# A gated mixing block on one Trainium2 core: the last plain columns of the input projection join the two-by-two scheme, and x's sums of squares come from rows

## The chip, the core and the metric

The kernel runs on one core of a Trainium2 chip. Five engines work side by side, each through its own list of instructions in order: TensorE (PE) multiplies matrices into eight accumulation banks; VectorE (DVE) and ScalarE (ACT) do elementwise work; GpSimd (POOL) does elementwise work too; SyncE (SP) issues most of the loads. An instruction waits until the ones that it depends on, on other engines or in DMA queues, have signalled. The metric is the time of one execution in microseconds (us) on the device, as the median of several runs.

## The reference, cut to what matters

```python
h = rms_norm(x, norm_mix_g) * (1.0 + sc1) + sh1           # sc1, sh1 from silu(c) @ w_ada
proj = einsum('bsd,de->bse', h, w_in)                     # 1024 tokens, 1024 -> 7168 columns
b_s, c_s, v_s, v_c, gl_c, gate_br = split(proj, ...)
y_a = (b_s * causal_dwconv3(c_s * v_s)) @ w_short_out
u   = causal_dwconv31(v_c * sigmoid(gl_c)) + bias
y_b = silu(layer_norm(u)) @ w_conf_out
g_a, g_b = split(sigmoid(gate_br))
x = x + g1 * ((g_a * y_a + g_b * y_b) @ w_o)
x = x + g2 * swiglu(rms_norm(x) * ... )                   # then a last rms_norm
```

The change is in the first two lines: the norm of x, and the projection.

## The kernel before

Channels lie on partitions. x, h and all products are tiles of 128 channels by 512 tokens: eight chunks of channels, two halves of tokens (0 and 1). A weight matrix is cut into blocks of 128 by 128. fp32 values are split into a rounded part and a rest, and each block product takes three matmuls (`mm3`, lines 293, 294, 296): weight high by data high, weight high by data rest, weight rest by data high. `split_w` makes the parts of a weight tile: the cast on ACT (L211), the rest on DVE or POOL (L212). Three tiles of each part exist, so a weight tile can be split once the matmuls of the third tile before it are over. The first `WHOLE` = 3 chunks of the lead are multiplied as plain fp32 instead (L289).

Most of the projection goes through *duals*: two pairs of 128 columns at a time, as a two-by-two block scheme with seven products in place of eight (`PRODUCTS` = "1265734" gives their order). The blocks of the weights are named 11, 12, 21, 22 (first or second column of the pair, first or second four chunks of channels); those of h are the four chunks of either half and either half of the tokens. Product 1 is the first column by the first four chunks of token half 0, product 2 the same column by the last four; together they are that column's result on half 0. Products 6, 5, 7, 3, 4 work on sums of blocks. Every product of a dual is 2 pairs x 4 chunks x 3 = 24 matmuls. Three banks for each pair, x, y and z, take turns. The weights' block sums and their rests are made by POOL (L235 to L239, L212), the data's sums and splits by DVE and ACT (`t_split`, L332 and L333). `PAIRS` lists which columns make the pairs: "u" is a channel block of the convolution branch with its sigmoid gate, "p" a block of c_s and v_s, "q" one of b_s, "g" output gates.

Ahead of the twelve duals stands the *lead*: the three first "u" blocks and one gate column, seven columns in seven banks, by all eight chunks, on token half 0 and then on half 1 (`row_blocks`). `act_x` makes a chunk of h when it is due: two loads and reductions of the modulation weights ada (L274), the scale (L360), the shift and split (L364 to L372). After the lead one more gate column is done plainly (`col_block`, tile gb). The norm needs the sum of squares over channels, which lie on partitions: ACT squares each chunk, DVE adds the eight (L404, L408), and a matmul with ones sums over partitions into every row of a bank (L414); the inverse root is refined on 128x512 tiles (L343 to L350).

The order of the work is set by the program's order and a scheduler in the recording layer, within explicit constraints (`issue_after`). `plan` lists the weight tiles; `next_w` keeps `AHEAD` = 2 of them ready. Raw weights pass through five buffers; a load starts when the tile that held its buffer is used up, and SP issues loads in order. The 31-tap convolution is DVE work that is spread over the duals: `paced` ties every tap to a moment counted in products (`CONV_DUALS`). Tiles "uc" (eight, of a whole token length) hold u, p, sc and loads of ada; tiles "gs" (six half-wide ones) hold evacuated products. After the duals follow the y_a stage (the short branch's output projection, also in seven products), y_b, mix, the ffn and the last norm, whose code stays as it is but for the y_a stage's order.

Of the kernel before, what the change touches and what calls it, by code (L numbers as in the profile page):

```python
# [39 lines left out]
P = 128  # L40
# [24 lines left out]
LEAD = 7  # L65
WHOLE = 3


X1_AT = 5
# [14 lines left out]
CONV_DUALS = 10.8  # L84
MOD_DUALS = 9
AT_READS = {"7": 4.5, "3": 5.5, "4": 6.5}
# [25 lines left out]
def block_kernel(ctx: ExitStack, tc: tile.TileContext, x0, xT, c, vecs, ada, w_first, w_plain, w_duals,  # L112
# [63 lines left out]
    aff2 = cp.tile([P, KC], F32, name="aff2")  # L176
    wsum = cp.tile([P, CK // 2 * KC], F32, name="wsum")
# [22 lines left out]
    pool_los = []  # L200
# [4 lines left out]
    def split_w(raw, n, after=(), lo_engine=nc.vector):  # L205
        wh = whp.tile([P, 1024], F32R, tag="wh", name="wh")[:, :n]
        wl = wlp.tile([P, 1024], F32R, tag="wl", name="wl")[:, :n]
        with ExitStack() as order:
            for ins in after:
                order.enter_context(tc.issue_after(ins))  # L210
            nc.scalar.copy(wh, raw)  # L211
            lo = lo_engine.tensor_tensor(wl, raw, f32(wh), ALU.subtract)  # L212
        if n == T and lo_engine is nc.gpsimd:
            pool_los.append(lo.ins)
        return wh, wl

    def dual_units(mats, n, early=False, eng=nc.vector, lo=None):
# [6 lines left out]

        def unit(m):
            if early:
                get(*{"1": ("11",), "2": ("12",), "6": ("21", "22", "11"), "3": ("12",), "4": ("22",)}.get(m, ()))
            elif m == "1":
                get("11", "12", "21", "22")
            los = (lo or {}).get(m, eng)  # L230
            if m in "12":
                return split_w(a["1" + m], n, (), los)
            if m == "6":
                a["s1"] = a["22"] if early else raw_tile(n)
                eng.tensor_tensor(a["s1"], a["21"], a["22"], ALU.add)  # L235
                eng.tensor_tensor(a["21"], a["21"], a["11"], ALU.add)
                eng.tensor_tensor(a["11"], a["11"], a["s1"], ALU.add)
            elif m == "3":
# [3 lines left out]
        return {m: (lambda m=m: unit(m)) for m in PRODUCTS}  # L242


    plan = [None] * KC
    plan += [(w_plain[0], 1024)]
# [1064 lines left out]
```

## Time and profile before

| | us |
|---|---|
| median of 3 runs | 1485.38 (1481.1 to 1486.36) |
| the profiled execution | 1482.34 |
| its span | 1480.6 |
| first matmul of the lead | 18.74 |
| lead, token half 0 | 18.74 to 63.96 |
| lead, token half 1 | 63.96 to 102.05 |
| the plain gate column | 102.05 to 112.93 |
| twelve duals | 112.93 to 570.00 |

In a row of the timeline stand the start, the duration, the engine, the line, the operation, the tile written and the tiles read with their shape, and in brackets how long the engine stood idle before and what ended that. In a row of waits stand who waited for whom, the sum, the number of times and the longest. A row of windows gives the stretch, its length, then for PE, weight loads, DVE, ACT and POOL the busy time and the number of instructions, the clock granted to PE, the DMA engines' mean share and what they moved in GB/s. A row of one tile's view gives an operation's count and its shortest, median and longest duration in ns.

### The profile page before, as it was taken

What the parts mean: (1) busy time and instruction counts of PE and PEld (TensorE: products, weight loads), DVE (VectorE), ACT (ScalarE), POOL (GpSimd) and SP (SyncE); (2) the same over time, 40 slices, a digit from 0 to 9 for tenths busy, and PEclk for the clock granted to TensorE, in tenths of its full rate; (3) what the DMA queues carried; (4) which work ended last, traced back from release to release, by engine and by line L of the source; (5) the groups of instructions that cost most, each with busy time, mean ns of one, the idle gap of its engine ahead of it and who ended that gap; (6) DMA issues with size and microseconds to landing.
All of it is one profiled execution on the core that took longest, in us unless ns stands there. A gap on an engine that the chain in (4) does not pass through costs nothing.

```text
span 1480.6 us, 17737 instructions
## 1 busy us (share of the span) xinstructions
PE 1454.6 (98%) x6407; PEld 1189.3 (80%) x6407; DVE 1184.1 (80%) x1626; ACT 641.8 (43%) x926; POOL 528.1 (36%) x468
## 2 busy tenths in 40 slices
PE   6999999999999999999999999999999999999997
PEld 2788888888888888878888778888888888888887
DVE  7994999889999979989588699877676765677755
ACT  4663434444333346455336465444444443222235
POOL 0027777776877673110022001111000116545005
PEclk9999999999999999999999999999999999999999
DMA  9623223233322345575476338655444449998403
GB/s 351 219 75 100 91 89 120 93 107 122 107 71 72 107 133 201 200 221 189 159 262 210 118 107 264 238 187 177 140 158 145 139 156 351 375 298 269 157 4 114
DMA packets 84858, 247.78 MB, mean 167 GB/s; under 512 B 9761, under 2 KB 11937, under 8 KB 84770
## 3 DMA queue, kind: packets, MB, share of 16 engines
q1 hardware_dynamic: 40768, 134.24, 27.5%
q0 software_dynamic: 38096, 99.63, 20.3%
q10 hardware_dynamic: 5906, 12.78, 2.2%
q8 instruction: 50, 0.82, 0.2%
q14 instruction: 38, 0.31, 0.1%
HBM read 186.31 MB, written 60.29 MB: 167 GB/s over the span
## 4 chain that ended last, share of the span: by engine, by line
PE 86%; DVE 6%; issue 3%; DMA 2%; POOL 2%; ACT 0%; POOLq 0%; ACTq 0%; DVEq 0%
PE x L293 10%; PE x L294 10%; PE x L296 10%; PE z L294 7%; PE z L296 7%; PE z L293 7%; PE y L296 6%; PE y L294 6%; PE y L293 6%; PE yb L294 2%; PE mix L293 2%; PE yb L296 2%; PE mix L294 2%; PE mix L296 2%; PE yb L293 2%
## 5 line engine op out<-in xcount | busy, mean ns | idle before, releaser
L211 ACT CAST wh<-raw 128x1024 fp32r<-128x1024 f32 (+2 forms) x263 | 265.6, 1010 | 405.6 <-PE z L294 112.9
L212 POOL TENSOR_TENSOR wl<-raw,wh 128x1024 fp32r<-128x1024 f32 x85 | 209.7, 2471 | 108.4 <-ACT wh L211 108.4
L212 DVE TENSOR_TENSOR wl<-raw,wh 128x1024 fp32r<-128x1024 f32 (+2 forms) x178 | 204.4, 1149 | 49.5 <-ACT wh L211 47.9
L703 DVE SCALAR_TENSOR_TENSOR c<-diff,vec,c 128x512 f32<-128x512 f32 x248 | 176.6, 751 | 2.2
L1028 POOL DMA_DIRECT2D hid<-stage x71 | 37.8, 533 | 334.7 <-DVE stage L333 330.1
L293 PE MATMUL x<-th,wh 128*128 128x512 f32 x240 | 93.4, 389 | 0.0
L294 PE MATMUL x<-tl,wh 128*128 128x512 f32 x240 | 93.4, 389 | 0.0
L296 PE MATMUL x<-th,wl 128*128 128x512 f32 x240 | 93.4, 389 | 0.0
L703 DVE SCALAR_TENSOR_TENSOR c<-u,wsum,c 128x512 f32<-128x512 f32 x112 | 84.0, 750 | 2.0 <-ACT c L707 0.4
L332 ACT CAST stage<-g 128x512 fp32r<-128x512 f32 x62 | 38.4, 622 | 65.8 <-DMA hid<-stage 32.3
L293 PE MATMUL z<-th,wh 128*128 128x512 f32 x168 | 65.4, 389 | 0.0
L294 PE MATMUL z<-tl,wh 128*128 128x512 f32 x168 | 65.4, 389 | 0.0
L296 PE MATMUL z<-th,wl 128*128 128x512 f32 x168 | 65.4, 389 | 0.0
L235 POOL TENSOR_TENSOR raw<-raw 128x1024 f32<-128x1024 f32 x12 | 29.8, 2483 | 95.3 <-DVE wl L212 94.5
L333 DVE TENSOR_TENSOR stage<-g,stage 128x512 fp32r<-128x512 f32 x62 | 42.5, 689 | 24.4 <-ACT stage L332 24.4
L274 DVE CUSTOM_DVE_ANT_0 ada<-ada,cs,vec 128x1024 f32<-128x1024 f32 x33 | 49.0, 1500 | 9.0 <-DMA ada<-in_ada 9.0
L1054 POOL DMA_DIRECT2D th<-hid x71 | 38.1, 536 | 46.5 <-PE x L296 25.1
L293 PEld LDWEIGHTS x<-th,wh 128*128 128x128 f32 x240 | 45.0, 188 | 9.4
L296 PEld LDWEIGHTS x<-th,wl 128*128 128x128 f32 x240 | 45.0, 188 | 9.4
L294 PEld LDWEIGHTS x<-tl,wh 128*128 128x128 f32 x240 | 45.0, 188 | 9.2
L293 PE MATMUL y<-th,wh 128*128 128x512 f32 x132 | 51.3, 389 | 0.0
L294 PE MATMUL y<-tl,wh 128*128 128x512 f32 x132 | 51.3, 389 | 0.0
(923 smaller groups left out, 4273.5 us busy)
## 6 DMA issues: line engine op xcount, KB each, us to landing
hid<-stage POOLq DMA_DIRECT2D x71, 512.0 KB, 4.4
raw<-in_w_fi SPq DMA_DIRECT2D x53, 512.0 KB, 3.9
raw<-in_w_duals SPq DMA_DIRECT2D x48, 512.0 KB, 3.6
th<-hid POOLq DMA_DIRECT2D x71, 256.0 KB, 5.9
tl<-hid POOLq DMA_DIRECT2D x71, 256.0 KB, 6.2
ada<-in_ada SPq DMA_DIRECT2D x33, 512.0 KB, 5.3
raw<-in_w_fo SPq DMA_DIRECT2D x24, 384.0 KB, 6.2
raw<-in_w_conf SPq DMA_DIRECT2D x16, 512.0 KB, 4.4
```

The source lines that it names most:

```text
L211: nc.scalar.copy(wh, raw)
L212: lo = lo_engine.tensor_tensor(wl, raw, f32(wh), ALU.subtract)
L235: eng.tensor_tensor(a["s1"], a["21"], a["22"], ALU.add)
L274: nc.vector.tensor_tensor_reduce(out=raw, in0=raw, in1=cs, scale=1.0, scalar=col(V_ADA, b), op0=ALU.mult, op1=ALU.add, accum_out=modc(b),)
L293: nc.tensor.matmul(ps, wh, xh, start=first, stop=False, skip_group_check=again)
L294: nc.tensor.matmul(ps, wh, xl, start=False, stop=False, skip_group_check=again)
L296: mm3.ins = nc.tensor.matmul(ps, wl, xh, start=False, stop=last, skip_group_check=again).ins
L332: nc.scalar.copy(hi, src)
L333: t_split.ins = nc.vector.tensor_tensor(lo, src, f32(hi), ALU.subtract).ins
L703: tap.ins = nc.vector.scalar_tensor_tensor(out=out, in0=src[:, s : s + H], scalar=wt, in1=acc, op0=ALU.mult, op1=ALU.add).ins
L1028: nc.gpsimd.dma_start(hid_dram[key], s)
L1054: nc.gpsimd.dma_start(t, hid_dram[key][:, s])
```

## The change

All 28 column pairs now go through fourteen duals. The lead is no longer three whole "u" blocks and a gate but the *first columns* of the first seven pairs, and it runs on token half 0 alone. After four chunks the banks hold product 1: ACT copies them away (`m1_store`), those of dual 0 to tiles that stay, the others to DRAM; then the banks go on and hold products 1 + 2, which is the column's result on half 0 (`first_out`). Products 1 and 2 of the remaining first columns of duals 3 to 5 follow as products *ahead*, while the second half's norm and the block sums are made (`h1_pair`). A dual below 6 then copies its kept product 1 into its bank and runs only products 6, 5, 7, 3, 4. Its weights are loaded block by block when a product needs them (`early`), the block 22 a second time, since its buffer takes a sum.

For the norm a second copy of x, `xt`, comes with tokens on partitions. The sum of squares of a token is then a sum along a row that the squaring instruction gives itself (`row_square`): ACT does three of the four tiles of half 0, DVE one. The inverse root is made for four columns of 128 tokens, each column is spread to a diagonal matrix on ACT, and one matmul with ones puts it into every row of a bank (`row_spread`, `row_sum`), where the modulation reads it.

Also changed: the modulation loads of the duals are issued in duals 3 to 11 in place of 0 to 8; the convolution is paced from product 5 to 77.6 of 86 in place of 0 to 75.6 of 84; in the y_a stage an evacuation is issued only after the splits of the two next ready weight tiles, and two of the eight loads of the convolution's results come three products later.

```diff
-    ("p", 0), ("g", ("b", 2), ("b", 3)), ("p", 1), ("u", 3), ("q", 0), ...
+    ("u", 0), ("u", 1), ("u", 2), ("g", ("b", 0), ("b", 1)), ("p", 0), ("g", ("b", 2), ("b", 3)),
+    ("p", 1), ("g", ("b", 4), ("b", 5)), ("u", 3), ("g", ("b", 6), ("b", 7)), ("p", 2), ...
...
-CONV_DUALS = 10.8
+AHEAD_DUALS = 6
+CONV_FROM, CONV_TO = 5, 77.6
+MOD_FROM = 3
...
+    def row_square(h, i, t, act=True):
+        ss = rcol[h][0][:, i : i + 1]
+        if act:
+            return nc.scalar.activation(t, t, AF.Square, scale=1.0 / 32.0, accum_out=ss).ins
+        return nc.vector.tensor_tensor_reduce(
+            out=t, in0=t, in1=t, scale=1.0 / D, scalar=0.0, op0=ALU.mult, op1=ALU.add, accum_out=ss
+        ).ins
+    def row_spread(h, act):
+        ss, r, t = rcol[h]
+        with tc.issue_after(act):
+            nc.scalar.activation(r, ss, AF.Abs_reciprocal_sqrt, bias=eps1)
+        rstd_end(ss, eps1, r, t, None)
+        spread = g_tile("spread")
+        for i in range(H // P):
+            nc.scalar.activation(spread[:, i * P : (i + 1) * P], ident, AF.Copy, scale=r[:, i : i + 1])
+        return spread
+    def row_sum(spread):
+        bank = ps2_tile("rx")
+        nc.tensor.matmul(bank, ones, spread, start=True, stop=True)
+        return bank
...
+    def m1_store(d, p, ps):
+        t = hl_tile("m1", dt=F32)
+        m1_ins.append(nc.scalar.copy(t, ps).ins)
+        if d == 0:
+            m1[d, p] = t
+            return
+        m1_dram[d, p] = dram.tile([P, H], F32, name=f"m1_{d}{p}")
+        nc.scalar.dma_start(m1_dram[d, p], t)
...
+        xs, w = ops[k]
+        for o in range(LEAD):
+            mm3([lead[o]], slice(o * P, o * P + P), w, [xs], k == 0, k % KH == KH - 1, k >= KH)
+            if k == KH - 1:
+                m1_store(o // 2, o % 2, lead[o])
             elif k == KC - 1:
+                first_out(o // 2, o % 2, lead[o])
...
+    steps = [(d, m) for m in "12" for d in range(LEAD // 2, AHEAD_DUALS)]
+    for i, (d, m) in enumerate(steps):
+        if 0 < i <= KH:
+            h1_pair(i - 1)
+        w = next_w()
+        for p in range(d == LEAD // 2, 2):
...
+            (m1_store if m == "1" else first_out)(d, p, ahead[d, p])
+        if i == 0:
+            with tc.issue_after(mm3.ins):
+                rx_1 = row_sum(spread)
...
+        if d < AHEAD_DUALS:
+            for p in range(2):
+                nc.scalar.copy(x[p], m1[d, p])
+        for m in PRODUCTS[2 if d < AHEAD_DUALS else 0 :]:
...
+            with ExitStack() as order:
+                for ins in [e for r in ready[:2] for e in made[id(r[1])]]:
+                    order.enter_context(tc.issue_after(ins))
```

The lists of three engines show what moves. First ACT at the start, from its first square to the scale that releases the lead (sq and rx0r are the squares and the inverse root; rc are the columns of row sums, wh and wl here the tiles that hold the rows). Before:

```order
L404 ACTIVATE sq<-x_128 128x512 x2
L404 ACTIVATE sq<-x_130 128x512 x2
L404 ACTIVATE sq<-x_132 128x512 x2
L404 ACTIVATE sq<-x_134 128x512 x2
L458 ACTIVATE cs<-cb 128x512 x2
L356 ACT_TABLE_LOAD
L356 ACTIVATE rs<-ones 128x1
L343 ACTIVATE rx0r<-ss,eps_99 128x512
L364 ACTIVATE x_189<-x_189,mod 128x512
```

And now:

```order
L430 ACTIVATE wh,rc_111<-wh 128x1024 x2
L493 ACTIVATE cs<-cb 128x512 x2
L382 ACT_TABLE_LOAD
L382 ACTIVATE rs<-ones 128x1
L430 ACTIVATE wl,rc_111<-wl 128x1024
L439 ACTIVATE rc_112<-rc_111,eps_99 128x4
L443 ACTIVATE spread<-ident,rc_112 128x128 x4
L390 ACTIVATE x_186<-x_186,mod 128x512
```

Two row squares stand ahead of the two silu, one behind the table's load; the eight squares and the wide inverse root are gone.

Second ACT in the changed kernel where the first dual begins (ahead are the banks of the products ahead, sig a gate, x_885 and x_886 the first dual's banks, m1 the kept product 1, th the high parts of its operands):

```order
L220 CAST wh_774<-raw_461 128x1024
L554 DMA gate_b6_132<-sig_771 128x512
L549 COPY p2_790<-ahead_659 128x512
L358 CAST th_808<-x00_186 128x512
L553 ACTIVATE sig_805<-ahead_676 128x512
L728 COPY x_885<-m1_305 128x512
L554 DMA gate_a0_118<-sig_805 128x512
L358 CAST th_812<-x10_200 128x512
L728 COPY x_886<-m1_310 128x512
```

In the kernel before, the same place has only the evacuation of the plain column, and the first dual's bank is filled by PE itself:

```order
L211 CAST wh_989<-raw_756 128x1024
L438 ACTIVATE sig_912<-gb0_862 128x512
L438 ACTIVATE sig_915<-gb1_863 128x512
L439 DMA gate_b1_116<-sig_912 128x512
L439 DMA gate_b1_116<-sig_915 128x512
L653 COPY y_981<-x_979 128x512
```

The copies of the kept product, which the first dual's matmuls add to, now stand behind the sigmoid of the last bank ahead.

Third POOL's weight work in an early dual. Before, one whole dual's list from its last two rests of the dual before (raw are the weight blocks and their sums, wl the rests that PE multiplies):

```order
L212 TENSOR_TENSOR wl_1090<-raw_758,wh_1089 128x1024
L212 TENSOR_TENSOR wl_1122<-raw_762,wh_1121 128x1024
L235 TENSOR_TENSOR raw_1233<-raw_1157,raw_1159 128x1024
L236 TENSOR_TENSOR raw_1157<-raw_1157,raw_1153 128x1024
L212 TENSOR_TENSOR wl_1162<-raw_1153,wh_1161 128x1024
L237 TENSOR_TENSOR raw_1153<-raw_1153,raw_1233 128x1024
L212 TENSOR_TENSOR wl_1195<-raw_1155,wh_1194 128x1024
L239 TENSOR_TENSOR raw_1155<-raw_1155,raw_1153 128x1024
```

Now the list of dual 1 from the rest of its product 7 (wl_1074) through those of its products 3 (wl_1109) and 4 (wl_1143); raw_1179, 1181, 1183 and 1288 are blocks 21, 22, 11 and 12 of dual 2:

```order
L221 TENSOR_TENSOR wl_1074<-raw_998,wh_1073 128x1024
L243 TENSOR_TENSOR raw_1181<-raw_1179,raw_1181 128x1024
L244 TENSOR_TENSOR raw_1179<-raw_1179,raw_1183 128x1024
L221 TENSOR_TENSOR wl_1109<-raw_1105,wh_1108 128x1024
L245 TENSOR_TENSOR raw_1183<-raw_1183,raw_1181 128x1024
L258 TENSOR_TENSOR raw_1288<-raw_1288,raw_1183 128x1024
L221 TENSOR_TENSOR wl_1143<-raw_1140,wh_1142 128x1024
```

All four adds of the next dual now stand between the rests of products 7 and 4 of the running one. raw_1181 has the buffer of raw_998, and raw_1288 that of raw_1105, so each of the two loads can start only when the row above that reads the old tile is done.

More of the change, by code (lines that the diff above doesn't have):

```diff
@@ L445, in block_kernel, with x0_load @@
     nc.scalar.activation(cp.tile([P, 1], F32, name="si"), ones[:, :1], AF.Silu)
+    rows = [f32(p.tile([P, D], F32R, tag=n, name=n)) for n, p in (("wh", whp), ("wl", wlp)) for _ in range(2)]
+    for i, t in enumerate(rows):
+        nc.sync.dma_start(t, xt[i])
     xin = {}
-    for k in range(0, KC, 2):
+    def x0_load(k):
         t = uc_tile("x0", T)
```

296 lines of the change are left out of this document (156 added, 140 removed), and 7 rows, old and new, of the table PAIRS.

## The prediction

> **What bounds the kernel now.** I read the page's busy shares first, then the list of what TensorE (PE) waited for, then the stages by windows, then the timelines of the start and of the weight splits.
>
> ```profile
> PE 1454.6 (98%) x6407; PEld 1189.3 (80%) x6407; DVE 1184.1 (80%) x1626; ACT 641.8 (43%) x926; POOL 528.1 (36%) x468
> ```
> ```profile
> PE ss L414 <- DVE sq L408: 6.1, 1, 6.1
> PE lead L289 <- ACT x L364: 4.6, 1, 4.6
> PE cb L454 <- DMA diff<-in_c: 2.3, 1, 2.3
> ...
> PE yb L294 <- DVE zsl L325: 1.2, 1, 1.2
> PE z L293 <- DVE v L826: 0.7, 1, 0.7
> ```
> ```profile
> 18.74:63.96 45.22, 45.22 (x150) 28.89 (x150) 41.48 (x73) 23.64 (x34) 0.00 (x0) 1.00 0.78 293
> 63.96:102.05 38.09, 38.09 (x169) 31.40 (x168) 38.03 (x50) 24.51 (x38) 5.51 (x2) 1.00 0.34 101
> 102.05:112.93 10.88, 10.88 (x50) 9.01 (x49) 8.45 (x11) 6.96 (x12) 6.32 (x3) 1.00 0.07 26
> 112.93:570.00 457.07, 456.89 (x2015) 377.66 (x2014) 406.71 (x566) 186.38 (x258) 340.79 (x147) 1.00 0.30 102
> ```
>
> PE is busy 98% of 1480.6 us at a granted clock of 1.00. Its only large waits lie before the first projection matmul at 18.74. From there to the end of the twelve duals at 570.00 it hardly stops, so a matmul less is time less, unless a new wait appears. The last window gives the price: 12 duals x 168 = 2016 matmuls in 457.07 us, 0.2267 us each, 5.44 us for a product of 24.
>
> **The matmuls.** The seven lead columns and the plain column cost 16 column-halves x 8 chunks. In duals, four such pairs take seven products in place of eight. The lists of PE fall from 6370 matmuls to 6322; the 21 fp32 ones of the first three chunks stay. 48 x 0.2267 = **-10.9 us**.
>
> **The start.**
>
> ```profile
> 4.42 1.15 ACT L404 ACTIVATE sq<-x 128x512 f32<-128x512 f32 x2 [1.24 <-DMA x<-in_x]
> 6.08 1.15 ACT L404 ACTIVATE sq<-x 128x512 f32<-128x512 f32 x2 [0.51 <-DMA x<-in_x]
> ...
> 8.77 1.15 ACT L404 ACTIVATE sq<-x 128x512 f32<-128x512 f32 x2 [0.18 <-DMA x<-in_x]
> 9.83 1.06 ACT L458 ACTIVATE cs<-cb 128x512 f32<-128x512 f32 x2
> 10.91 1.28 ACT L356 ACT_TABLE_LOAD   x1
> 12.21 0.20 ACT L356 ACTIVATE rs<-ones 128x1 f32<-128x1 f32 x1
> ...
> 17.96 0.72 ACT L364 ACTIVATE x<-x,mod 128x512 f32<-128x512 f32 x1 [3.06 <-DVE x L360]
> ```
> ```profile
> 6.58 5.47 DVE L408 TENSOR_TENSOR sq<-sq 128x512 f32<-128x512 f32 x7
> 11.97 1.28 DVE L274 CUSTOM_DVE_ANT_0 ada<-ada,cs,vec 128x1024 f32<-128x1024 f32 x1
> ...
> 14.38 0.16 DVE L280 SCALAR_TENSOR_TENSOR aff<-mod,vec 128x1 f32<-128x1 f32 x1
> ...
> 17.18 0.75 DVE L360 SCALAR_TENSOR_TENSOR x<-x,aff,rx0r 128x512 f32<-128x512 f32 x1
> ```
> ```profile
> 12.11 2.08 PE L414 MATMUL ss<-sq,ones 128*128 128x512 f32 x2 [6.10 <-DVE sq L408]
> 18.74 20.43 PE L289 MATMUL lead<-x,raw 128*128 128x512 f32 x42 [4.56 <-ACT x L364]
> ```
>
> The four rows arrive as the four loads did, the last at 8.77. ACT squares two rows (at most 1.15 each, the price of two halves; to 7.2), does both silu (1.06; 8.3), the table (1.28) and its dummy (0.20; 9.8), then the fourth row (10.9); the third is DVE's. The inverse root is now of four columns (0.20), and its three DVE steps are too (about 0.2 each, from the one-column row of 0.16; 11.8). Four 128x128 spreads follow: each between 0.20 (one column) and 0.53 (a half of the silu pair); I take 0.25, nearer the small one since they are a quarter wide (12.8). Then one summing matmul (2.08; 14.9), the modulation (0.75) and ACT's bias (0.72): PE starts at 16.5, **-2.2 us** (-2.6 to -1.1 with those ends). One more 512 KB load stands before the first ada loads; loads land 1.3 to 1.7 us apart, so the second ada lands near 12.8 and its reduction (1.28) ends at 14.1, hidden under the 14.9. Without that cover each late us is lost.
>
> **New waits on PE.** (1) ACT must copy the seven lead banks after chunk 3, before chunk 4 adds to them. A column of three matmuls takes 0.68 us, so PE is back at the seventh bank 12 columns, 8.2 us, after it left the first. ACT needs seven copies, one bias step (0.72) and four stores issued between them.
>
> ```profile
> 561.44 0.33 ACTq L564 DMA_DIRECT2D gate_a<-v  x1
> 561.88 1.05 ACT L211 CAST wh<-raw 128x1024 fp32r<-128x1024 f32 x1 [0.47 <-ACT v L563]
> ```
> ```profile
> 577.74 0.60 ACT L818 COPY y<-x 128x512 f32<-128x512 f32 x1
> ```
>
> A store blocks ACT for 0.33 to 0.47: 7 x 0.60 + 0.72 + 1.6 = 6.5 us. It begins some 2 us late, behind chunk 5's cast, whose turn DVE's pace sets: 8.5 against 8.2, **+0.3** (0 to 1.4). (2) At the first dual's product 6, its kept product is copied into the bank by ACT behind the sigmoid of the very last product ahead: two ACT steps of 0.60 in a row with PE idle, **+1.2** (0.6 to 1.8). Later duals use a spare bank and load early: 0.
>
> (3) Duals 1 to 5 have five products on POOL, no longer seven, and their weight loads come one by one.
>
> ```profile
> L211 ACT CAST wh<-raw x37: 1037/1052/1057, 129.4 to 325.2; 128x1024 fp32r<-128x1024 f32 x37
> L212 POOL TENSOR_TENSOR wl<-raw,wh x37: 2390/2409/3434, 130.5 to 326.3; 128x1024 fp32r<-128x1024 f32 x37
> ...
> DMA to landing us min/median/max: 3.4/3.6/4.9
> ```
>
> From a dual's start: product 7's split waits for the slot that product 4 of the dual before just left (cast 1.05, POOL 2.41, ends at 3.5); only that frees the buffer for the next dual's block 22 (load 3.6; 7.1). POOL's order puts two adds and product 3's split next (3 x 2.43; 14.4); that split frees block 12's buffer (18.0), and the add that needs it stands ahead of product 4's split (22.9). PE asks for that split at 4 x 5.44 + 2 x 0.23 = 22.2. So 0.7 us in duals 1 to 3; in dual 4 the split stands before the adds (7.1 + 6 x 2.43 = 21.7, no wait): **+2.1** (0 with loads of 3.4 and a gap less; +10 with loads of 4.9).
>
> [...]
>
> **What I cost at nothing.** The second token half's normalization moves into the ahead products: 8 modulations, 16 block sums, 4 splits and four weight splits (one of half width) on DVE between the second rsqrt's matmul and the first dual. The old stage has the prices:
>
> ```profile
> 61.26 1.41 DVE L360 SCALAR_TENSOR_TENSOR x<-x,aff,rx1r 128x512 f32<-128x512 f32 x2
> ...
> 82.22 0.69 DVE L523 TENSOR_TENSOR x<-x,x 128x512 f32<-128x512 f32 x1
> 82.82 0.69 DVE L337 SCALAR_TENSOR_TENSOR x<-t,x 128x512 f32<-128x512 f32 x1
> ...
> 94.22 1.22 DVE L212 TENSOR_TENSOR wl<-raw,wh 128x1024 fp32r<-128x1024 f32 x1
> ...
> 137.75 0.69 DVE L613 TENSOR_TENSOR v<-x,v 128x512 f32<-128x512 f32 x1 [18.62 <-issue]
> ```
>
> A modulation follows the next after 0.67, a half-wide step after 0.60, a weight split after 1.14: 5.4 + 20 x 0.60 + 4 = 21 us beside 24.5 us of matmuls. Covered with 3 us over; without cover PE waits for each us. The rest is moved work: DVE was 406.71 of 457.07 us busy in the duals and gets some nine more half-wide steps (5 us), while the 18.62 us that it stood idle ahead of the first conv are now mostly open to it. The conv still ends 8.4 products before the duals do (7 x 10.8 of 84, now 77.6 of 86). The DMA queues carry some 16 MB more (rows, two duals, reloaded blocks, kept products) and 4 MB less of lead and plain weights. After the lead the share is 0.34 and less, so that hides. In the lead it is the tightest resource:
>
> ```profile
> 20.00:40.00 20.00, 20.00 (x46) 8.95 (x46) 18.84 (x34) 7.67 (x10) 0.00 (x0) 1.00 0.96 359
> ```
>
> 22.4 MB must land by the second modulation, near 65 us; at 359 GB/s that is 62 us. Every us beyond 65 would be PE's. In the y_a stage the evacuations are now held behind weight splits and the loads cut in two; the waits there (0.7 and 1.2 above) hang on an ada load and on the second norm; I keep them, between 2 us less and 2 us more.
>
> **The sum.** -10.9 - 2.2 + 0.3 + 1.2 + 2.1 = **-9.5 us**. The profiled execution took 1482.34 us (1480.6 and 1.7 around it), so 1472.8. The median of the runs is 1485.38, 3.0 above it; on that scale 1475.9. I say 1476.
>
> **Rivals.**
> *The loop is covered.* Loads at 3.4 us and a spare gap or two suffice; -11.5 us, 1474, or 1472 if the y_a waits go too. For it: 1.1 of the 22.9 us need to go. Against: POOL's longest steps are 3.4 us.
>
> *DVE falls behind before and in the first dual.*
> ```profile
> 108.43 10.70 DVE L333 TENSOR_TENSOR tl<-x,th 128x512 fp32r<-128x512 f32 x6 [2.21 <-ACT th L332]
> ```
> ```profile
> 109.02 2.73 POOL L237 TENSOR_TENSOR raw<-raw 128x1024 f32<-128x1024 f32 x1
> 111.71 2.85 POOL L212 TENSOR_TENSOR wl<-raw,wh 128x1024 fp32r<-128x1024 f32 x1
> 114.64 2.73 POOL L239 TENSOR_TENSOR raw<-raw 128x1024 f32<-128x1024 f32 x1
> ```
> ```profile
> 579.04 2.49 DVE L325 TENSOR_TENSOR tql<-q,tqh 128x512 fp32r<-128x512 f32 x4
> ```
> Six splits took 1.78 us each beside POOL, where four took 0.62 each alone. After the change POOL's four adds for dual 1 (4 x 2.75 = 11 us) fall among the last block sums and the first dual's splits: DVE does 6 steps for 18 and loses 7 us; some 2 us of slack remain, so PE loses 5: -4.5 us, 1481. Against: the splits have two products' lead by then. [...]
>
> *The start is not earlier*, because loads share the DMA engines with one more in front, or the row squares' sums cost extra steps: -7.3 us, 1478.
>
> *POOL's loop runs slow*, and the time is longer. If its steps in duals 1 to 4 run at 2.9 us (between the 2.41 median and 3.43 longest) and both loads take 4.9, the loop gains 5 x 0.5 + 2.6 us on 0.7: 5.8 us x 4 = 23 us, -11.6 + 23 = +11.5, 1497. It eats the whole gain from 2.9 us per dual on.
>
> **Chances.** Forecast 0.42 (own range 1473 to 1479), loop covered 0.25, DVE behind 0.15, start unchanged 0.10, POOL slow 0.08. A difference of 0.5%, 7.4 us, is about what a measurement here can tell from none. Faster than that: 0.36 of the forecast's 0.42 and 0.25: 0.61; within: 0.06 + 0.15 + 0.10 = 0.31; slower 0.08. The range runs from 1470 (loop covered, y_a waits gone, and 2 us of spread between runs) to 1484 (DVE behind, and the same spread).
>
> **What will show it.** PE's first lead matmul at 16.5; lead over after 44 us more; a PE wait of some 1.2 us on ACT's copy of the kept product near 90 us; waits of 0.7 us on POOL's wl once in each of the duals 1 to 3, near 140, 168 and 196 us; duals over near 560.5, against 570.00. Wrong if PE waits on DVE's tl or t2l between 75 and 115 us, if the first dual starts after 93, or if the POOL waits sum to over 5 us.

## The result, and the profile after

| | before | after |
|---|---|---|
| median of 14 runs | 1482.60 us (1480.95 to 1486.36) | 1488.33 us (1482.26 to 1493.27) |
| span of the profiled execution | 1480.6 | 1486.5 |
| first matmul of the lead | 18.74 | 16.84 |
| first matmul on split operands | 38.60 | 36.23 |
| duals over (first matmul of the mean) | 570.77 | 571.80 |
| second sum of squares | 833.59 | 837.58 |
| last sum of squares | 1470.37 | 1475.93 |

The ratio after to before is 1.0035, with a 95% interval from 1.0022 to 1.0049: a little slower, by some 5 us, where 9.5 us less was forecast. The range ended at 1484.

First the stages by windows, cut at the moments of the table, of the kernel before and then of the changed one.

```profile
18.74:38.60 19.86, 19.86 (x42) 8.71 (x43) 18.70 (x34) 6.95 (x9) 0.00 (x0) 1.00 0.93 349
38.60:570.77 532.17, 531.99 (x2342) 438.87 (x2340) 476.73 (x666) 235.11 (x332) 352.62 (x151) 1.00 0.32 107
570.77:833.59 262.82, 260.00 (x1132) 211.72 (x1130) 210.84 (x299) 129.35 (x184) 38.86 (x72) 1.00 0.62 207
833.59:1470.37 636.78, 635.03 (x2882) 527.15 (x2883) 463.11 (x601) 258.68 (x381) 130.96 (x233) 1.00 0.58 190
```
```profile
16.84:36.23 19.39, 19.39 (x42) 8.56 (x43) 17.32 (x31) 6.09 (x8) 0.00 (x0) 1.00 1.03 408
36.23:571.80 535.57, 525.21 (x2293) 432.02 (x2292) 467.97 (x669) 245.22 (x358) 356.04 (x152) 0.99 0.40 133
571.80:837.58 265.78, 261.30 (x1133) 212.93 (x1131) 214.16 (x302) 129.41 (x184) 40.42 (x73) 0.99 0.62 208
837.58:1475.93 638.35, 635.88 (x2881) 527.09 (x2882) 464.25 (x601) 259.24 (x381) 130.93 (x233) 1.00 0.59 189
```

The second rows hold the case. The matmuls listed from one cut to the next are 2339 before and 2291 after (a window counts those that it touches at its ends too): the 48 are gone, 48 x 0.2267 = 10.9 us, as forecast. Yet the stretch is 3.4 us longer. The 2291 would take 519.4 us, so 16.2 us are not matmuls at full pace, against 1.9 before. The gain was made, and 14.3 us of new losses took it. Outside: -2.4 us up to the first split matmul, +3.0 in the y_a, y_b and mix stages, +1.6 in the ffn, +0.3 at the end. In all 3.4 - 2.4 + 3.0 + 1.6 + 0.3 = 5.9 us, the difference of the spans.

What PE waited for in the changed kernel, from the list of waits:

```profile
PE rx L449 <- ACT spread L443: 6.0, 1, 6.0
PE x L322 <- POOL wl L221: 3.8, 1, 3.8
...
PE y L322 <- POOL wl L221: 3.2, 2, 1.8
PE z L322 <- DVE wl L221: 1.9, 1, 1.9
...
PE z L322 <- POOL wl L221: 1.6, 1, 1.6
PE lead L315 <- ACT x L390: 1.6, 1, 1.6
PE y L319 <- ACT wh L220: 1.4, 1, 1.4
PE x L319 <- ACT x L728: 1.2, 1, 1.2
...
PE x L320 <- DVE tl L359: 0.6, 1, 0.6
```

The four waits on POOL's wl are new, 8.6 us. They are the loop of the early duals, one in each of the duals 1 to 4, as the timeline of PE has them:

```profile
142.26 0.50 PE L322 MATMUL y<-th,wl 128*128 128x512 f32 x1 [1.76 <-POOL wl L221]
...
173.03 0.50 PE L322 MATMUL z<-th,wl 128*128 128x512 f32 x1 [1.63 <-POOL wl L221]
...
204.34 0.64 PE L322 MATMUL x<-th,wl 128*128 128x512 f32 x1 [3.82 <-POOL wl L221]
204.78 0.63 PE L319 MATMUL x<-th,wh 128*128 128x512 f32 x1
205.21 0.63 PE L320 MATMUL x<-tl,wh 128*128 128x512 f32 x1
...
234.84 0.50 PE L322 MATMUL y<-th,wl 128*128 128x512 f32 x1 [1.40 <-POOL wl L221]
```

Behind the third wait the matmuls follow one another at 0.43 us, not 0.23. The windows around the first and the third wait (the clock is the third number from the end) show why:

```profile
143.20:146.60 3.40, 3.40 (x10) 2.63 (x9) 0.93 (x2) 0.33 (x1) 3.40 (x2) 0.51 0.92 253
146.60:150.00 3.40, 3.40 (x17) 2.78 (x16) 3.12 (x5) 1.20 (x2) 0.28 (x1) 1.00 0.82 287
...
204.34:207.77 3.43, 3.43 (x8) 2.66 (x9) 0.99 (x2) 0.51 (x2) 3.43 (x2) 0.53 0.70 168
```

After a wait PE can run for 3.4 us at half the granted clock (0.51 and 0.53 in these windows). That costs eight matmuls 0.2 us each, 1.6 us more, which no list of waits shows. It happened twice in the early duals and once in the y_a stage. So the loop cost 9.6 us of waits (the four, with 0.15 to 0.3 us of restart around each) and 3.2 us at half pace: 12.8 us. With the copy of the kept product (1.4 with its restart) and the wait on tl (0.8), less 0.8 of small gaps that only the kernel before had, that is the 14.3 to within 0.1.

### The profile page after: what moved, and what is told of

It is laid out like the page before. It is cut to its first block, busy times and chain, and to the rows that moved or that the text cites. A ratio compares the mean times of both kernels' runs of the same rounds, so it can differ in the third digit from the quotient of the medians.

```text
span 1486.5 us, 17733 instructions
## 1 busy us (share of the span) xinstructions
PE 1449.5 (98%) x6359; PEld 1183.5 (80%) x6359; DVE 1173.4 (79%) x1624; ACT 651.3 (44%) x954; POOL 533.5 (36%) x471
## 4 chain that ended last, share of the span: by engine, by line
PE 69%; issue 18%; POOL 4%; DVE 4%; DMA 3%; ACT 1%; POOLq 0%; SPq 0%; DVEq 0%; ACTq 0%
PE x L319 9%; PE x L320 9%; PE x L322 9%; PE z L322 6%; PE z L319 6%; PE z L320 6%; PE y L322 6%; PE y L319 6%; PE y L320 6%; POOL wl L221 1%; PE lead L315 1%; DMA raw<-in_w_duals 1%; DMA hid<-stage 1%; DVE wl L221 1%; POOL x_dram L980 1%
## 5 line engine op out<-in xcount | busy, mean ns | idle before, releaser
L220 ACT CAST wh<-raw 128x1024 fp32r<-128x1024 f32 (+3 forms) x262 | 264.5, 1010 | 383.6 <-PE x L320 114.2
L221 DVE TENSOR_TENSOR wl<-raw,wh 128x1024 fp32r<-128x1024 f32 (+2 forms) x180 | 208.2, 1158 | 60.2 <-ACT wh L220 58.2
L221 POOL TENSOR_TENSOR wl<-raw,wh 128x1024 fp32r<-128x1024 f32 x82 | 209.2, 2558 | 89.2 <-ACT wh L220 89.2
L322 PE MATMUL x<-th,wl 128*128 128x512 f32 x304 | 119.0, 391 | 3.8 <-POOL wl L221 3.8
L320 PE MATMUL x<-tl,wh 128*128 128x512 f32 x304 | 118.9, 391 | 0.6 <-DVE tl L359 0.6
L319 PE MATMUL x<-th,wh 128*128 128x512 f32 x304 | 119.0, 391 | 0.0
L322 PE MATMUL z<-th,wl 128*128 128x512 f32 x216 | 84.1, 390 | 1.6 <-POOL wl L221 1.6
L320 PE MATMUL z<-tl,wh 128*128 128x512 f32 x216 | 84.0, 389 | 0.0
L319 PE MATMUL z<-th,wh 128*128 128x512 f32 x216 | 84.0, 389 | 0.0
L322 PE MATMUL y<-th,wl 128*128 128x512 f32 x180 | 70.9, 394 | 3.2 <-POOL wl L221 3.2
L319 PE MATMUL y<-th,wh 128*128 128x512 f32 x180 | 70.8, 393 | 0.0
L320 PE MATMUL y<-tl,wh 128*128 128x512 f32 x180 | 70.6, 392 | 0.0
L243 POOL TENSOR_TENSOR raw<-raw 128x1024 f32<-128x1024 f32 x13 | 33.0, 2542 | 96.7 <-DVE t2l L359 79.8
```

Of the source, the lines that this page charges most:

```text
L220: hi = nc.scalar.copy(wh, raw)
L319: nc.tensor.matmul(ps, wh, xh, start=first, stop=False, skip_group_check=again)
L320: nc.tensor.matmul(ps, wh, xl, start=False, stop=False, skip_group_check=again)
L322: mm3.ins = nc.tensor.matmul(ps, wl, xh, start=False, stop=last, skip_group_check=again).ins
```

## The experiments

The ratios are to the kernel before on the same chip. e1 to e4, e5 to e8 and e9 to e11 ran on three chips; the medians of the kernel before on them are 1482.70, 1483.05 and 1482.70 us, so medians from different chips can be compared to within some 0.4 us. "Duals over" and "stage" (from the mean's matmul to the second sum of squares) are of the profiled execution.

| kernel | median us (runs) | ratio to before, 95% interval | span | duals over | stage |
|---|---|---|---|---|---|
| changed kernel | 1488.33 (14) | 1.0035 (1.0022 to 1.0049) | 1486.5 | 571.80 | 265.78 |
| e1, product 4's rest on DVE | 1495.87 (5) | 1.0083 (1.0070 to 1.0096) | 1493.9 | 575.42 | 270.59 |
| e2, POOL's add behind the rest | 1479.79 (11) | 0.9979 (0.9969 to 0.9988) | 1475.8 | 562.57 | 264.34 |
| e3, y_a order as before | 1490.20 (5) | 1.0048 (1.0036 to 1.0060) | 1488.5 | 570.57 | 268.99 |
| e4, small reloads of kept products | 1487.34 (11) | 1.0037 (1.0023 to 1.0051) | 1487.9 | 572.00 | 266.15 |
| e5, last sum earlier | 1486.25 (12) | 1.0022 (1.0010 to 1.0035) | 1484.5 | 570.94 | 264.23 |
| e6, e2 and e5 | 1476.96 (5) | 0.9958 (0.9946 to 0.9970) | 1475.3 | 562.89 | 264.71 |
| e7, e1 with the sums' list kept | 1479.92 (10) | 0.9981 (0.9969 to 0.9993) | 1478.4 | 563.57 | 265.92 |
| e8, e6, modulation loads later | 1476.97 (5) | 0.9956 (0.9944 to 0.9968) | 1476.6 | 561.03 | 265.04 |
| e9, e6 and e3 | 1480.55 (9) | 0.9981 (0.9971 to 0.9991) | 1479.1 | 562.46 | 269.40 |
| e10, e6 with four waits put in | 1494.41 (2) | 1.0076 (1.0058 to 1.0094) | 1491.6 | 579.91 | 264.31 |
| e11, e7 and e5 | 1478.03 (5) | 0.9965 (0.9952 to 0.9977) | 1474.3 | 560.75 | 265.21 |

### The loop: two rows of POOL's list change places (e2)

```diff
             if m == "3":
-                eng.tensor_tensor(a["12"], a["12"], a["11"], ALU.add)
+                with ExitStack() as order:
+                    if early and eng is nc.gpsimd and last4:
+                        order.enter_context(tc.issue_after(last4[-1]))
+                    eng.tensor_tensor(a["12"], a["12"], a["11"], ALU.add)
...
+            if m == "4" and early and eng is nc.gpsimd:
+                last4.append(made[id(out[1])][1])
```

> Edit: on GpSimd, the add for the next dual's block 12 is issued behind the running dual's rest of product 4, no longer ahead of it; nothing else moves. Theory A1 (what PE waits for is the load of block 12, behind which product 4's rest stands in GpSimd's queue): that rest then starts when the add before it ends (near 135.0 in dual 1, where now 139.84), is ready near 137.5, 3 us before PE asks for it at 140.5, and the waits of duals 1 to 3 go; in dual 4 one step of 2.4 us fewer stands ahead of it and the wait of 1.40 goes too: duals over near 559.5. Theory A2 (GpSimd has too many steps in a dual, whatever their order): the wait moves to the next product, and at most half of the 12.8 us comes back.

POOL's timeline in dual 1, of the changed kernel and then of e2 (L243 to L245, and L258 or here L261, are the adds; the three L221 are the rests of products 7, 3 and 4):

```profile
119.28 2.40 POOL L221 TENSOR_TENSOR wl<-raw,wh 128x1024 fp32r<-128x1024 f32 x1 [1.32 <-ACT wh L220]
125.41 2.41 POOL L243 TENSOR_TENSOR raw<-raw 128x1024 f32<-128x1024 f32 x1 [3.73 <-DMA raw<-in_w_duals]
127.90 2.40 POOL L244 TENSOR_TENSOR raw<-raw 128x1024 f32<-128x1024 f32 x1
130.26 2.42 POOL L221 TENSOR_TENSOR wl<-raw,wh 128x1024 fp32r<-128x1024 f32 x1
132.62 2.42 POOL L245 TENSOR_TENSOR raw<-raw 128x1024 f32<-128x1024 f32 x1
137.48 2.40 POOL L258 TENSOR_TENSOR raw<-raw 128x1024 f32<-128x1024 f32 x1 [2.44 <-DMA raw<-in_w_duals]
139.84 2.38 POOL L221 TENSOR_TENSOR wl<-raw,wh 128x1024 fp32r<-128x1024 f32 x1
```
```profile
130.35 2.42 POOL L221 TENSOR_TENSOR wl<-raw,wh 128x1024 fp32r<-128x1024 f32 x1
132.71 2.44 POOL L245 TENSOR_TENSOR raw<-raw 128x1024 f32<-128x1024 f32 x1
135.06 2.45 POOL L221 TENSOR_TENSOR wl<-raw,wh 128x1024 fp32r<-128x1024 f32 x1
137.69 2.41 POOL L261 TENSOR_TENSOR raw<-raw 128x1024 f32<-128x1024 f32 x1 [0.17 <-DMA raw<-in_w_duals]
```

In the changed kernel POOL stands idle for 2.44 us before the add, since block 12 has not landed, and the rest that PE asks for stands behind that add. In e2 the rest starts at 135.06 and is ready at 137.5; the add comes at the same time as before, 137.69, and nobody misses it. The waits of duals 1 and 2 are gone, the one of dual 3 too; two of 1.1 and 1.4 us are left in dual 4 (on the rests of products 3 and 4, after POOL waited 5.5 us for a block 22), so the duals end at 562.57, 9.2 us earlier (12.3 were expected). Theory A1 holds: POOL had the time, its order did not. The median is 8.5 us below that of the changed kernel, and 2 parts in 1000 below the kernel before.

### Whose work it is (e1, e7)

e1 gives product 4's rest to DVE: `{m: nc.vector for m in "124"}` in place of `"12"` in the plan's line for the early duals.

> Edit: in duals 1 to 5 the rest of product 4's weights is made by VectorE in place of GpSimd. Theory A (the weight loop of the early duals costs PE its waits: in the changed kernel 1.76, 1.63, 3.82 and 1.40 us, and behind two of them 1.5 and 1.7 us of matmuls at half pace): all four waits go, GpSimd's queue no longer holds what PE asks for, and the end of the duals moves from 571.8 to about 559.5; the span falls by 12 us, to about 1474. Theory B (VectorE is so full in the duals that five more steps of 1.2 us come back as waits on the data's splits or on the convolution): the four waits are replaced by others and the duals end within 4 us of 571.8.

The waits on POOL in duals 1 and 2 went. In duals 3 and 4 two of 1.9 and 1.7 us came in place of the old ones, now on the rest of product 3, which is still POOL's. Others are new: five on ACT's copy of a product 1 (L737; 1.6, 1.3, 2.8, 1.5 and 1.3 us) and one of 5.0 us in the y_a stage. The duals ended 3.6 us later. By the expectation Theory B had won. But the edit did a second thing: `add_conv` ties POOL's sums of the convolution (tot += u, L809) to the n-th entry of `pool_los`, the list of the splits that POOL makes, and five splits had left that list. The last sum came at 568.03, not 553.54. e7 makes the same edit with those five splits still counted in the list.

> Edit: as in the first experiment VectorE makes the rest of product 4's weights in the early duals, but these splits keep their place in the list by which GpSimd's sums are timed. Theory G (the first experiment lost because its sums of the convolution came some 14 to 25 us later still, 232 to 568 against 209 to 554, and held buffers): the waits on the copy of product 1 (1.62, 1.30, 2.76, 1.51, 1.34) and the one of 5.00 in the y_a stage go, GpSimd's waits in duals 1 and 2 stay away, duals over within 3 us of 562.6, the span near 1476 to 1479. Theory B (VectorE is too full for these five steps): duals over later than 569 still.

The duals end at 563.57; of the five waits on L737 one (2.3 us) is left, the 5.0 is gone, and no wait on POOL's wl remains. The two kernels differ in the list alone, and their medians by 16 us. So Theory G holds but for that one wait: DVE had room for the five steps, and the sums' timing made e1 slow. It also showed where to look in the changed kernel itself.

### The sums' list in the change (e5)

The change too took splits off POOL: dual 0's five are DVE's. The trace has 85 splits of POOL up to 575 us before and 82 after, while the entry's number is worked out as a product's number, of 84 before and of 86 now, which counts dual 0's five. The last sum's entry went from 77 to 79, from the eighth last split to the third last. These rows are POOL's split and sum, SP's reload of the last q block, and DVE's two steps around its longest idle time, in the changed kernel:

```profile
551.20 2.39 POOL L221 TENSOR_TENSOR wl<-raw,wh 128x1024 fp32r<-128x1024 f32 x1 [2.80 <-ACT wh L220]
553.54 2.53 POOL L809 TENSOR_TENSOR tot<-tot,u 128x512 f32<-128x512 f32 x2
...
556.10 0.33 SPq L659 DMA_DIRECT2D q<-q  x1
...
548.30 0.69 DVE L363 SCALAR_TENSOR_TENSOR t<-q,sc 128x512 f32<-128x512 f32 x1 [2.16 <-DMA gate_a<-sig]
560.25 0.69 DVE L351 TENSOR_TENSOR tql<-q,tqh 128x512 fp32r<-128x512 f32 x1 [11.26 <-ACT tqh L350]
```

Before, these were

```profile
529.71 2.55 POOL L723 TENSOR_TENSOR tot<-tot,u 128x512 f32<-128x512 f32 x2
...
532.28 0.33 SPq L569 DMA_DIRECT2D q<-q  x1
```

The sum reads the last convolution result, so it holds that buffer; SP's reload waits for the buffer, and DVE for the reload. The edit:

```diff
-        with tc.issue_after(pool_los[min(int(CONV_FROM + (CONV_TO - CONV_FROM) * (j + 1) / KC) + 2, ...
+        with tc.issue_after(pool_los[min(int(CONV_FROM + (CONV_TO - CONV_FROM) * (j + 1) / KC) + (2 if j < KC - 1 else -2), ...
```

> Edit: GpSimd's last sum of a convolution result (tot += u, block 7) is tied to the split four places earlier in its list; nothing else. Theory E (that sum, at 553.5 in the changed kernel against 529.7 before, holds the buffer of the last q block; its reload is issued at 556.1 against 532.3, VectorE stands idle for 11.3 us in the last dual, and what it has not done then makes the waits of the y_a stage): the reload is issued near 536, VectorE is no longer idle for more than 3 us between 545 and 560, and the waits of the y_a stage (1.88, 1.44, 0.53, with 1.5 us at half pace) fall to those of the kernel before (0.29, 0.72, 1.18 in all) or less: the second sum of squares some 3 us earlier, near 834.6, the span near 1483. Theory F (the stage's waits have their cause in the stage): within 1 us of 837.6.

Now (SP, then DVE's windows over 540 to 560 of e5 and of the changed kernel):

```profile
537.14 0.33 SPq L659 DMA_DIRECT2D q<-q  x1
...
540.00:560.00 20.00, 20.00 (x19) 1.00 0.41 135
```
```profile
540.00:560.00 20.00, 6.83 (x8) 1.00 0.44 147
```

The reload is 19 us earlier and DVE is busy all of these 20 us, where it was for 6.8. The three waits of the y_a stage (1.9, 1.4, 0.5, with their half pace) are gone. But four others stand at its end (1.0, 1.2, 1.5 and 0.3). They come to 4.1 us, where the three were 3.9, so in sum the waits did not fall. The stage is 1.6 us shorter, which is about what its half pace had cost. The medians are 2.1 us apart, with intervals that overlap. Theory E holds as far as the reload and DVE's idle time; that these made the waits of the y_a stage is not shown, since others of the same length took their place.

### Both (e6), and three things around it (e8, e9, e11)

> Edit: both the order of GpSimd's add of block 12 behind the rest of product 4, and the earlier last sum. If the two causes are independent, the gains add: duals over near 562.6 and the y_a stage 3 us shorter, the span near 1473, the ratio to the kernel before 0.995 to 0.996. If the earlier end of the duals had already taken the y_a waits' cause away, the span stays near 1476.

1476.96 us, 0.9958 of the kernel before: 6 us faster than it and 11 faster than the change. From the profile of e2 to that of e6 the gain is 0.5 us only; but the profiled execution of e2 (1477.5) is one of its quickest, and the medians are 2.8 us apart. So the gains add in the medians, though the intervals of e2 and e6 still touch, and the profiles do not show it.

> Edit: the two fixes (order, last sum), and the y_a stage's evacuations and loads as in the kernel before. With the two causes gone, Theory L (the stage's new order was still a cost or nothing): the stage, from the mean's matmul to the second sum of squares, takes no more than the 264.7 us that it takes with the two fixes; the span is 1473 to 1475. Theory M (the new order is worth what it was in the third experiment, where undoing it made the stage 3.2 us longer): the span is 1477 to 1479.

Undoing the y_a order on top costs 3.6 us in the median and makes the stage 4.7 us longer (a wait of 4.4 on DVE's v, with twice 3.4 us at half pace around its end). On the change alone the same edit was

```diff
-                for ins in [e for r in ready[:2] for e in made[id(r[1])]]:
+                for ins in []:
...
-        if i in (0, 3):
-            for j in range(*((0, 6) if i == 0 else (6, KC))):
-                cv_load(j)
+        if i == 0:
+            for j in range(KC):
+                cv_load(j)
```

> Edit: in the y_a stage the evacuations are no longer held behind the splits of the two next weight tiles, and the eight loads of the convolution's results are issued together again, as in the kernel before. Theory C (this edit made the waits of the stage, 1.88, 1.44 and 0.53 us with 1.5 us at half pace, against 0.29, 0.72 and 1.18 before): the second normalization's sum of squares comes near 834.7 in place of 837.6, and the span falls by about 3 us. Theory D (the waits come from where the convolution's end and the loads fall, which the duals set): the stage stays within 1 us of what it was.

Theory C falls, and Theory D too: the stage grew to 268.99 with waits of 3.6, 0.9, 0.5, 1.5 and 1.2 us. Twice, undoing this part of the change cost 3.2 to 4.7 us of the stage. The medians are clear of noise for e9 against e6 alone; the intervals of e3 and the changed kernel overlap. So this part is a gain, of 3.6 us by the medians of e6 and e9.

> Edit: both fixes, and the modulation loads go with duals 5 to 13 in place of 3 to 11, so that none falls into the early duals. Theory H (in dual 4 the two loads of ada beside the reload of block 22, 5.4 us from issue to use, make the two waits that the order left, 1.12 and 1.43): they go, and the span is 2.5 to 3 us below that of the two fixes alone. Against: the last of these loads then fall into duals 12 and 13, where they compete for buffers with the reload of the q blocks; then what is won in dual 4 is lost behind 530.

The duals end 1.9 us earlier, but the wait in dual 4 is the same (0.71 against 0.68), and what was won does not reach the end: the y_a stage, with a wait of 3.7 on DVE's v, takes 0.3 us more than in e6, and the ffn 2.9 more, with a wait of 2.1 on DVE's g. The median is that of e6. Theory H isn't borne out for the wait. Most of the loss is later than the expectation had it, in a stretch that differs by up to 3 us between the runs, so that the edit made it is not shown.

The traces of e6 and e8 show one thing that these loads do cost. In e6 the rest of product 3 takes POOL 3.4 us in duals 3 and 4; in e8, where no reduction of ada falls beside it there, no step of POOL's weight work in duals 1 to 4 takes over 2.9 us. In the changed kernel the same pair stands in dual 3 (DVE, then POOL) and again in dual 4:

```profile
188.57 3.38 DVE L300 CUSTOM_DVE_ANT_0 ada<-ada,cs,vec 128x1024 f32<-128x1024 f32 x1
...
190.83 3.39 POOL L221 TENSOR_TENSOR wl<-raw,wh 128x1024 fp32r<-128x1024 f32 x1
```

> Edit: VectorE makes the rest of product 4 in the early duals, with the sums' list kept and the last sum earlier, and GpSimd's order as in the change. If what remains of the loop with the order alone (0.68 us in dual 4) is all that GpSimd costs, this gains nothing over the two fixes: 1475 to 1478 in span. If VectorE's five steps push the convolution's work back, it is 2 to 4 us slower than the two fixes.

1478.03: with intervals that overlap those of e6, no gain over the reordering. What e6 still loses to POOL in the early duals, 0.68 us, leaves little to win there.

### Is it the kept products' reload? (e4)

In dual 1 the reload of block 22 takes 3.5 us from issue to landing, that of block 12 takes 4.6 (the profile's rows of those single issues, in this order):

```profile
raw<-in_w_duals SPq DMA_DIRECT2D x1, 512.0 KB, 3.5
...
raw<-in_w_duals SPq DMA_DIRECT2D x1, 512.0 KB, 4.6
```

Behind the second, SP issues the two reloads of the kept products, which are new. The edit loads 64 of their 512 columns:

```diff
-            nc.sync.dma_start(m1[d, p], m1_dram[d, p])
+            nc.sync.dma_start(m1[d, p][:, :64], m1_dram[d, p][:, :64])
```

> Edit: in duals 1 to 5 the two kept products are reloaded with 64 of their 512 columns (an eighth of the bytes), the rest of the bank is filled from another tile, so part of the result is left out; the issues stay where they are. Theory A3 (the reload of block 12, 4.8 to 5.4 us from issue to landing in duals 1 to 3, is slowed by the two 256 KB reloads issued 0.4 and 0.8 us behind it; the reload of block 22, issued alone, takes 3.7 to 4.3): it lands in about 3.7 us, and the waits of duals 1 to 3 shrink by some 1.1 us each, to 0.7, 0.5 and 2.7, those on which the half pace hangs below it or nearly: duals over 3.3 to 6.5 us earlier, near 567. Theory A4 (the load is late for another reason): waits as before.

Block 12 landed in 4.9 us in dual 1, and the waits were 1.9, 1.7, 2.0 and 3.5 us. Theory A3 falls; the bytes of these reloads are not what makes that load slow. The issues stayed, but dual 4 of the changed kernel has the same two behind its block 12, which landed in 3.6 us. What differs is a row in the profile's list of DMA queues. From the issue of block 12 in dual 1 to its landing the list has

```profile
q8 instruction: 1, 0.02, 1.7%
```

which is one transfer of 16 KB that took 1.30 us. From that of block 12 in dual 4 on there is none, and the issues are

```profile
raw<-in_w_duals SPq DMA_DIRECT2D x1, 512.0 KB, 3.6
m<-m SPq DMA_DIRECT2D x2, 256.0 KB, 4.0
```

In the twelve traces of kernels with these reloads 35 landings of a block 12 can be read. Their packets move from some 0.9 us after the issue on. The 12 without a transfer of the instruction queue in that time took 3.5 to 4.0 us, one beside a short transfer of 0.31 us took 4.1, and the 22 beside one of 0.88 to 2.26 us took 4.3 to 5.1. It is not a matter of the dual: in dual 2 of e1 and e11, without such a transfer, block 12 landed in 3.7 and 3.6 us. In the changed kernel such a transfer stands beside block 12 in each of the duals 1 to 3. So the late landings go with it, in e4 as well (1.69 us in dual 1); no run was made without it, so that it is the cause is likely and not shown.

### A wait costs more than its length (e10)

```diff
+            for _ in range(extra):
+                lo_engine.tensor_tensor(wl, raw, raw, ALU.subtract)
             lo = lo_engine.tensor_tensor(wl, raw, f32(wh), ALU.subtract)
```

with `extra` 5 for product 5 of duals 7 to 10, and 0 elsewhere.

> Edit: the two fixes, and in each of the duals 7 to 10 GpSimd makes five more steps of 2.4 us ahead of the rest of product 5 (into the tile that the rest then overwrites), so that PE stands still once in each, for 3 to 6 us. Theory J (a wait costs more than its length: where PE idled more than about half of some 3.4 us, the next 3.4 us go at half the granted clock and cost 1.6 us more): behind each of the four waits stand seven to nine matmuls at 0.43 us each, and the duals end later by the sum of the waits plus 6 to 7 us. Theory K (the half pace in the changed kernel had another cause, and a wait costs its length): later by the sum of the waits alone.

PE waited 3.76, 1.55, 2.19 and 3.59 us in duals 7 to 10, where 3 to 6 were aimed at, and 1.78 in dual 4. These are the windows behind the five, in order of time:

```profile
221.03:224.40 3.37, 3.37 (x10) 2.65 (x9) 3.33 (x7) 0.59 (x1) 3.29 (x3) 0.54 0.80 305
319.90:323.30 3.40, 3.40 (x10) 2.67 (x9) 3.33 (x3) 1.03 (x2) 3.25 (x2) 0.53 0.72 233
360.10:363.50 3.40, 3.40 (x15) 2.83 (x16) 3.26 (x5) 0.59 (x1) 3.40 (x2) 1.00 0.60 164
401.70:405.10 3.40, 3.40 (x10) 2.69 (x9) 3.22 (x6) 0.58 (x1) 3.40 (x2) 0.51 0.80 211
444.20:447.60 3.40, 3.40 (x15) 2.80 (x16) 3.40 (x6) 0.72 (x1) 3.40 (x2) 1.00 0.67 163
```

Three of the five were followed by 3.4 us at half the clock, two were not. The duals end 17.0 us later than in e6. The five waits with their restarts are 14.2, the three stretches 4.7, and 1.8 us that e6 lost elsewhere did not occur here: 17.1. Theory K, by which the waits alone would have been lost, falls. Theory J holds, but not for every wait: one of 1.78 us brought it on, one of 3.59 did not.

## Why the prediction was wrong

| step of the sum | forecast | measured |
|---|---|---|
| the matmuls | -10.9 | -10.9 (2339 to 2291 at 0.2267) |
| the start | -2.2 | -1.9 at the first matmul, -2.4 at the first split one |
| (1) copies of the lead banks after chunk 3 | +0.3 | 0: no gap over 0.1 us in the rest of the lead |
| (2) kept product behind the sigmoid | +1.2 | +1.2 at 89.92, 1.4 with its restart |
| (3) POOL's weight loop | +2.1 (0 to +10) | +12.8: 9.6 of waits, 3.2 at half pace |
| DVE before and in the first dual, "at nothing" | 0 | +0.8 (one tl, at 103.94) |
| the y_a stage, "between 2 us less and 2 us more" | 0 | +3.0 |
| ffn and end | 0 | +1.9 |
| small gaps that only the kernel before had | 0 | -0.8 |

**The step that failed is (3), "0.7 us in duals 1 to 3".** The mechanism was the one described. With wl7, wl3 and wl4 for the rests of products 7, 3 and 4: wl7 frees block 22's buffer, wl3 frees block 12's, the add that needs block 12 stands ahead of wl4, and PE asks for wl4. The terms of its sum were too small. Block 12's load went in at 3.6 and the add could start 4.8, 4.7 and 5.4 us after wl3's end in duals 1 to 3 (landing, and the start behind it); block 22's went in at 3.6 and took 3.7, 3.7, 4.3 and, in dual 4, where no wait was forecast and 1.40 came, 4.75; and one split in each of the duals 3 and 4 took 3.39 us in place of 2.43, beside a reduction of ada. With these sizes the prediction's own sum gives waits of 2.0, 1.9, 4.1 and 1.6 us in duals 1 to 4; 1.8, 1.6, 3.8 and 1.4 were measured. The prediction named these prices as its upper end ("+10 with loads of 4.9") and took the lower one, the median landing in the kernel before. That was the median of loads issued in other company; no row showed these loads. In dual 1 two loads of one size, 512 KB, took 3.5 and 4.6 us. The 4.6 was beside the transfer of the instruction queue.

**What the sum lacked altogether is the half pace**: 3.2 us in the loop, 1.5 in the y_a stage. A wait was priced at its length.

The base was off as well: the forecast of 1476 stands on a median of 1485.38 from three executions, and fourteen gave 1482.60, so the same -9.5 us would have meant 1473.

**The rival that came true is the last one, POOL's loop runs slow**, with its place right and its price between: "it eats the whole gain from 2.9 us per dual on", and the loop cost 3.2 us per dual. Of its two causes the late loads came; POOL's steps stayed at 2.4 us but for the two of 3.39. It was given 8 in 100. The bounds stood there, 0 and 10, and the estimate was put a fifth of the way up with no row that was near these loads. The order of the two rows, which e2 shows to be worth 9 us, was quoted in the text ahead of the prediction. The rival that DVE falls behind was wrong: one wait of 0.6 us. The rival that the loop is covered asks for 1.1 us less where the prediction's own sum asks for 0.7; it failed for the same loads.

**The y_a stage** went by "the conv still ends 8.4 products before the duals do". The taps do, nearly: the last result is stored at 529.3 against 525.9 before. But POOL's sum of that result is timed by another count, the list of POOL's splits, which the change made shorter. It moved from 529.7 to 553.5, and with it a buffer, a reload and 11 us of DVE. e5 shows this much, and not that it cost the stage its 3.0 us; why the stage then has other waits, as long in sum, was not followed further. What its own edit brings was costed at nothing, and e3 and e9 show 3 to 5 us of gain. So something else makes the stage longer: with both fixes and without that edit (e9) it takes 269.4 us, 6.6 more than before. What it is stays open.

**The ffn's +1.6** is not explained. In the other runs this stretch, whose code none of them touches, took 636.7 to 640.0 us with no relation to the edits.

**Clock and time.** The 14 executions of the changed kernel differ by 11 us. Their mean granted clock goes with it: the two at 0.998 took 1482.3 and 1484.4 us, the six at 0.994 and 0.995 took 1488.3 to 1493.3. A clock lower by 0.004 over 1486 us is 5.9 us. The five of e6 lie at 0.998 and 0.999, within 1.6 us. So, as an estimate from these clocks, about half of that spread could be the half pace, on in one execution and off in another; which waits set it off in the executions without a profile can't be seen.

## What to carry to other kernels

Where a load stands in an engine's queue ahead of work that somebody waits for, price the load at the longest landing in the trace, not at the median, or move the work that waits for it behind: two rows of one list were worth 9 us here. The longest landing is no outlier to set aside when the same thing, here a transfer of the instruction queue, stands beside the load in dual after dual. When work moves from one engine to another, look for everything that is timed by counting that engine's instructions; the count shifts, and what is tied to it moves without a line of the diff showing it. A wait of TensorE of 1.76 us cost 1.6 us more than its length here, and one of 1.63 us did not, so several short waits can cost more than their list adds up to.

## What was not expected of the hardware

Stretches of 3.4 us at a granted clock of 0.51 to 0.54 follow some waits of PE and not others. In the changed kernel they came behind waits of 1.76 us, of 3.82, and of 1.44 with 0.53 1.3 us later; not behind 1.63, 1.40, 1.88 and 1.69. The granted clock in windows of 0.1 us puts the three stretches at 143.1 to 146.5, 204.6 to 208.0 and 627.8 to 631.2. Each is 3.41 us long, and their begins lie whole multiples of 3.413 us apart: 61.4 us is 18 of them, 423.2 is 124. If time is cut by that grid, the windows ahead of the three stretches were idle for 52%, 94% and 58% of their length, and those ahead of no stretch, from 25 us on, for at most 48%.

That fits a grid of 3.413 us that the waits do not shift, with a bound near half of a window, and the traces of all thirteen kernels bear it out. Between 25 us and the last matmul they have 19 windows at half pace, all on their trace's grid, and each stands behind a window that was idle for 52% or more. No window idle for 51% or less was followed by one, and every one idle for 58% or more was. Between 52% and 57% both happened: five windows were followed by half pace and four were not. The bound is no sharper than that here, for the ends of matmuls in the timeline are modelled. This also places the wait of 3.59 us in e10: the grid cut it into 57% of one window and 48% of the next, while the waits of 1.78, 3.76 and 2.19 us gave windows of 52%, 66% and 64%.

In e10 a wait of 1.78 us, half as long as a window, was enough, and a wait of 3.59, longer than a window but spread over two, left no slow matmul behind: where a wait falls mattered there as well as its length.
